# Norms and value parts that read the PSUM bank themselves, and buffers given back when their transfers should have landed

## The chip, the cores and the metric

The kernel runs on one core of a Trainium2 chip. A core has five engines that take instructions from queues of their own: TensorE (PE, matrix products into eight PSUM banks), VectorE (DVE), ScalarE (ACT), GpSimdE (POOL) and SyncE (SP), which here issues every DMA. The metric is the device time of one execution in microseconds (us). It was 2167.8 us, the median of three runs (2167.16 to 2171.36).

## The reference

One layer of a decoder runs over a prompt of 2048 positions and over 32 sample positions (8 sequences of 4 new tokens with caches). The input is RMS-normalised and projected by one wide matrix `w_in` to queries, keys, values, gates and mixing factors. Two attention branches read the projections:

- branch A: a causal window of 128, 8 query heads on 2 key/value heads, with a learned sink per head;
- branch B: three groups of 8 heads with (window, dilation) = (128, 1), (512, 4), (2048, 16), so that each query reads 128 keys, strided. The three outputs are weighted by their softmax denominators.

Queries and keys are normalised per head before use:

```python
def qk_norm(a, g, scale=1.0):
    a32 = a.astype(jnp.float32)
    y = a32 * lax.rsqrt(jnp.mean(a32 * a32, axis=-1, keepdims=True) + EPS)
    return (y * g.astype(jnp.float32) * scale).astype(a.dtype)
```

```python
s = jnp.einsum('nbqhgd,nbchd->nbhgqc', qb, kc, preferred_element_type=jnp.float32)
p, l, m = softmax_stats(s + bias, mask[None, :, None, None], sink)
o = jnp.einsum('nbhgqc,nbchd->nbqhgd', p, vc.astype(jnp.float32))
```

Both branches pass a SiLU gate and an up-projection, are merged by sigmoid factors, projected by `w_out` and added to the input. Besides the outputs, the last window rows of keys (after the norm and its gain) and values are returned for the caches: all 2048 rows of the group with dilation 16, 512 of the group with dilation 4, 128 of the others.

## The kernel before

**Split numbers.** Every float32 operand of a large product is written as the sum of two float16 parts, high and low, and a product is three float16 matmuls (high x high, high x low, low x high). `split` makes the parts: ACT writes the high part (L303), DVE subtracts it from the source for the low part (L306 or L308).

**Stages.** First the input is normalised and the mixing gates are computed (to about 390 us). Then come the three dilated groups, dilation 16, 4 and 1, with 16 tiles of 128 positions each; then branch A with the gates, also 16 tiles; then up- and output projections (from about 1800 us). In the dilation-16 group a tile attends only to itself (`nk` = 1), in the others mostly to two tiles of keys (`nk` = 2). In parallel with each group, the sample positions are attended from the caches, with products on POOL (L1172) and loads on SP.

**A tile.** `b_tile` gives a tile three projections: queries, keys, values. `proj` sums each in one PSUM bank with 24 matmuls of 512 columns (L259, the line of the helper `mm`). Five banks rotate among the projections and small transposes (`pbank`, `tbank`); in A, projections may hold only four of them (`most[0] = 4`). Scores use banks 3 and 4, values bank 7. When a bank is full, its chain starts:

- `q_chain` and `k_chain` call `norm`. ACT copies the bank into an SBUF buffer (L730) and the bank is given back; ACT squares that copy into scratch (L738); DVE sums per head (L740) and adds a constant (L741); POOL raises to the power -1/2 (L743) and, for queries, multiplies the gains in (L747); DVE multiplies the copy by the result (L751). The copy lies in `sq` for queries and `stK` for keys, the scratch and the later float16 parts in `qn` and `kn`.
- `parts` splits the result, and one DMA transpose (`SP.turn`, L167) turns it, queries into `QT`, keys into `KT`. `k_turn` then makes a second key layout with two DVE copies of half the partitions each (L773).
- If the tile's rows are returned, `k_rows` multiplies `stK` by the gain on POOL (L977) and stores it to DRAM.
- `v_chain` copies the bank to `stV` (L999), gives the bank back, waits for the tile before to have done its values, splits `stV` into one of two value buffers `VT`, and stores `stV` if the rows are returned.

`attend` then issues units of heads: scores (PE), bias and row maximum (DVE, L801), a scaling of the maxima (ACT, L810), exponentials (ACT, L815), split, a turn of the probabilities by DMA, and values (PE, 64-column matmuls). `finish` copies bank 7 and the softmax statistics into `Ut` (L1011, L1012), which is stored to DRAM.

**What sets the order.** The kernel is written as concurrent generators over a planned clock (`Clock`). The clock has a time at which each engine is free and an estimate of when a DMA lands (`ck.come`). A generator yields the planned time at which it wants to go on; whichever is due first emits its instructions next. The order of emission is the order in each engine's queue. Buffers and banks are guarded by planned locks (`sq_l`, `qn_l`, `kn_l`, `stK_l`, `Ut_l`, the banks' `lock`). The plan decides only the order: on the chip, an instruction waits by semaphores for whatever it really depends on, and all that is behind it in its engine's queue waits too. Before the change most locks of buffers under transfer are given back when the DMA is issued; `turn` waits until `ck.come`.

Of the kernel before, what the change touches and what calls it, by code (L numbers as in the profile page):

```python
# [13 lines left out]
F16 = mybir.dt.float16  # L14
# [6 lines left out]
P = 128  # L21
# [8 lines left out]
CW = 528  # L30
# [120 lines left out]
def hybrid_kernel(ctx, tc, xp, xs, ca, cb1, cb2, cb3, rel_bias, norm_gain, w_in, qga, kga, sinks, qgb, kgb,  # L151
# [541 lines left out]
    Ps = [cv(2, 512, dt=F16) for _ in range(2)]  # L693
    A_OP1 = cv.off
    Ut = cv(CW)
    stK, stV = cv(512), cv(512)
    A_OP0 = A_OP1 + 1024
    op = [arena[:, A_OP0:A_OP0 + 1024], arena[:, A_OP1:A_OP1 + 1024]]
    cv = Carve(A_OP0 + 1024)
    cb = cv(3, CW)  # L700
    SAMP = cv.off
    A_STV = A_OP1 + CW + 1024
    VTa = [x.rearrange("p a b -> p (a b)")[:, 640:].rearrange("p (a b) -> p a b", a=3) for x in VT]
    kv = kn[:, 128:384]

    sq_l, qn_l, kn_l, U_l, Ut_l, stK_l, stV_l, cb_l, fst_l = (Lock(ck) for _ in range(9))
    S_l, Sb_l, Ps_l, op_l = ([Lock(ck), Lock(ck)] for _ in range(4))
    PT_l = [Lock(ck) for _ in range(3)]
    unit_n = [0]
# [13 lines left out]
    start.scored = start.valued = start.finished = True  # L723
    start.biased = 4

    def norm(src, p0, n, nh, blk, scr, dst, gains=None, raw=None):


        if raw:
            A.activation(dst, src, AF.Copy)  # L730
            src = dst
            yield use("A", ta(nh * 64))
            raw[0].put()
            yield from raw[1].get()
        st = nst[p0:p0 + n, nrm_n[0] % 5]
        nrm_n[0] += 1
        s = scr[p0:p0 + n, :nh * 64]
        A.activation(s, src, AF.Square)  # L738
        yield use("A", ta(nh * 64))
        V.tensor_reduce(st[:, 0, :nh], heads(s), axis=AX.X, op=OP.add)  # L740
        V.tensor_scalar(st[:, 1, :nh], st[:, 0, :nh], 1.0 / 64, blk.epsc[p0:p0 + n], op0=OP.mult, op1=OP.add)  # L741
        yield use("V", tv(nh * 64) + 140)
        G.tensor_tensor(st[:, 2, :nh], st[:, 1, :nh], nhalf[p0:p0 + n].to_broadcast([n, nh]), op=OP.pow)  # L743
        f = use("G", 250 + 170 * nh)
        r = st[:, 2, :nh, None].to_broadcast([n, nh, 64])
        if gains is not None:
            G.tensor_tensor(heads(s), r, gains.to_broadcast([n, nh, 64]), op=OP.mult)  # L747
            f = use("G", tg(nh * 64))
            r = heads(s)
        yield f  # L750
        V.tensor_tensor(heads(dst), heads(src), r, op=OP.mult)  # L751
        yield use("V", tv(nh * 64))
# [16 lines left out]
    def k_turn(nh, dst, cur):  # L769
        x, y = (v[:, :, cur] for v in dst)  # L770
        yield from turn(x, kn, nh)
        for j in range(2):
            V.tensor_copy(y[64 - 64 * j:128 - 64 * j], x[64 * j:64 * j + 64])  # L773
            e = use("V", 33 * nh + 65)
        yield e

    def unit(t, y, n3, us, last):


        g, nk, cur = t.g, t.nk, t.cur  # L780
        w = nk * P
        nm, l, m = t.st[:, 0], t.st[:, 1], t.st[:, 2]
        xs_ = slice(2 * us[0], 2 * us[-1] + 2)
        hs = [(2 * u + j, u, j) for u in us for j in range(2)]
        sb = Sb[:, y]
        for a, (x, u, j) in enumerate(hs):
            for p_ in range(2):
                ks = t.KT[p_][:, x if g else j]
                ks = ks.rearrange("p s t -> p (s t)") if nk == 2 else ks[:, cur]
                mm(bank[3 + y][:, a * w:(a + 1) * w], t.QT[:, x], ks, p_ == 0, p_ == 1, cost(w))  # L790
        if last:
            t.scored = True
        yield ck.now + ck.LAT
        yield from Sb_l[y].get()
        for a, (x, u, j) in enumerate(hs):
            h = t.head(u, j)
            o, i_, b_ = sb[:, a * w:(a + 1) * w], bank[3 + y][:, a * w:(a + 1) * w], bias[:, h, (2 - nk) * P:]
            if nk == 2 and cur == 0:
                o, i_ = (v.rearrange("p (s t) -> p s t", s=2) for v in (o, i_))
                b_ = bass.AP(tensor=b_.tensor, offset=b_.offset + P, ap=[b_.ap[0], [-P, 2], [1, P]])  # L800
            V.tensor_tensor_reduce(out=o, in0=i_, in1=b_, scale=1.0,  # L801
                                   scalar=-3e38 if g else sinkS[:, u, j:j + 1], op0=OP.add, op1=OP.max,
                                   accum_out=m[:, x:x + 1])
            e = use("V", tv(w) + 80)
        t.used.update(us)
        while t.biased in t.used:
            t.biased += 1
        yield e
        S_l[y].put()
        A.activation(nm[:, xs_], m[:, xs_], AF.Copy, scale=ninv[:, g:g + 1])  # L810
        use("A", 200)
        t.nmd += len(us)
        for a, (x, u, j) in enumerate(hs):
            e = sb[:, a * w:(a + 1) * w]
            A.activation(e, e, AF.Exp, bias=nm[:, x:x + 1], scale=inv[:, g:g + 1], accum_out=l[:, x:x + 1])  # L815
            f = use("A", 0.833 * w + 372)
        yield f
        yield from Ps_l[y].get()
        yield from split(Ps[y][:, 0], Ps[y][:, 1], sb, 2.0 ** 14, 512)
        Sb_l[y].put()  # L820
        yield from PT_l[n3].get()
        pt = PT[n3]
        SP.turn(pt.rearrange("p b (a t) -> p (b a) t", t=P), Ps[y].rearrange("p b c -> p (b c)"))
        yield ck.come
        Ps_l[y].put()
        yield ck.now + 1800
        yield from cond(ck, lambda: t.v and t.prev.finished)
        for a, (x, u, j) in enumerate(hs):
            h = t.head(u, j)
            vc = (h if g else j) * 64  # L830
            o = bank[7][:, h * 64:h * 64 + 64]
            for n in range(nk):
                s = t.vslot(n if nk == 2 else cur)
                q = a * w + n * P
                ph, pl = (pt[:, z, q:q + P] for z in (0, 1))
                vh, vl = (t.VT[z][:, s, vc:vc + 64] for z in (0, 1))
                mm(o, ph, vh, n == 0, False, 27)
                mm(o, ph, vl, False, False, 27)
                mm(o, pl, vh, False, n == nk - 1, 27)
        PT_l[n3].put()  # L840
# [113 lines left out]
    def bcast_rows(row, n):  # L954
        return row[:, None, :].to_broadcast([n, 8, 64])

    def b_tile(g, t, tok, rows, nk, cur, last, par):
        t.g, t.nk, t.cur = g, nk, cur
        t.st = ast[:, par]
        t.QT, t.KT, t.VT = QT[(len(made) - 1) % 3], KT, VT  # L960
        t.head = lambda u, j: 2 * u + j
        t.vslot = lambda s: s
        prev = t.prev
        old = prev.prev and prev.prev.prev

        def q_chain(b):
            yield from sq_l.get()
            yield from norm(b.ap[:, :], 0, P, 8, blocks[f"q{g}"], qn, sq, GR[:, g % 2:g % 2 + 1], (b.lock, qn_l))
            yield from parts(qn, sq, 8, 1.0)
            sq_l.put()  # L970
            yield from cond(ck, lambda: old is None or old.scored)
            yield from turn(t.QT, qn, 8)
            qn_l.put()
            t.q = True

        def k_rows():
            G.tensor_tensor(heads(stK), heads(stK), bcast_rows(gk_row[:, g % 2], P), op=OP.mult)  # L977
            yield use("G", tg(512))
            SP.dma_start(rows[:, :512], stK)
            stK_l.put()  # L980
            t.kept = True

        def k_chain(b):
            yield from stK_l.get()
            yield from norm(b.ap[:, :], 0, P, 8, blocks[f"k{g}"], kn, stK, raw=(b.lock, kn_l))
            yield from parts(kn, stK, 8, 2.0 ** 11)
            if rows is None:
                stK_l.put()
# [5 lines left out]
            t.k = True  # L994

        def v_chain(b):
            yield from stV_l.get()
            blk = blocks[f"v{g}"]
            A.activation(stV, b.ap[:, :], AF.Copy, scale=2.0 ** -20 if rows is None else blk.c)  # L999
            yield use("A", ta(512, 1))  # L1000
            b.lock.put()
            yield from cond(ck, lambda: prev.valued)
            yield from split(VT[0][:, cur], VT[1][:, cur], stV, 1.0 if rows is None else blk.vs, 512)
            if rows is not None:
                SP.dma_start(rows[:, 512:], stV)
            stV_l.put()
            t.v = True

        def finish():
# [5 lines left out]
            def store():  # L1015
                yield e
                SP.dma_start(comb[g][tok], Ut)
                Ut_l.put()
                t.stored = True

            ck.spawn(store())
# [15 lines left out]
    sampB = samp_carve(A_STV, prod2=None)  # L1037
    cv = Carve(sampB["end"])
    KT.append(cv(8, 2, P, dt=F16))
    QT.append(cv(8, P, dt=F16))  # L1040
    sampA = samp_carve(SAMP, PT=A_PT, prod2=arena[:, A_SP:A_SP + 512],
                      Sr=arena[:, A_K + 1536:A_K + 1808])
# [311 lines left out]
    def a_tile(i, t, par):  # L1354
# [1 line left out]
        cur = i % 2  # L1356
        t.g, t.nk, t.cur = 0, 2 if i else 1, cur
        t.st = ast[:, par]
        t.QT, t.KT, t.VT = QT[1 - par], KTa, VTa
        t.head = lambda u, j: u + 4 * j  # L1360
        t.vslot = lambda s: (i if s == cur else i - 1) % 3
        t.ob = t.ga = t.gb = t.gs = t.cb = t.placed = False
        op_x = i % 2
        o = op[op_x]
# [22 lines left out]

        def q_chain(b):
            yield from sq_l.get()
            yield from norm(b.ap[:, :], 0, P, 8, blocks["q0"], qn, sq, GR[:, 0:1], (b.lock, qn_l))  # L1390
            yield from parts(qn, sq, 8, 1.0, True)
            sq_l.put()
            yield from cond(ck, lambda: prev.prev.scored)
# [453 lines left out]
```

## Time and profile before

| | before |
|---|---|
| median of three runs | 2167.8 us (2167.16 to 2171.36) |
| profiled execution: its time, its span | 2170.46 us, 2168.6 us |
| busy PE / DVE / ACT / POOL | 2029.2 / 1386.0 / 1053.3 / 707.9 us |
| mean granted TensorE clock | 0.979 |
| DMA | 344.34 MB, mean 159 GB/s |

A profile's span runs from the first to the last instruction. A row of a group names line, engine, operation, output and inputs, shapes and count; behind the bar stand total us and mean ns of one, behind the second bar the idle time of the engine just before, and what ended it. `arena` is the large SBUF buffer of which nearly all working buffers are parts, so `sq`, `stK`, `kn` and the rest all appear under that name; `bank` is a PSUM bank. In a timeline, a bracket gives the idle time before an instruction and what ended it. `SPq` is SP issuing a DMA.

### The profile page before, as it was taken

How to read it: one execution, taken by the hardware profiler on the slowest of the kernel's cores; microseconds unless marked ns; L12 is line 12 of the kernel's file. 1: busy time of each engine (PE TensorE's matmuls, PEld its weight loads, DVE VectorE, ACT ScalarE, POOL GpSimd, SP SyncE). 2: the span in 40 equal slices, each digit the busy share in tenths (PEclk: the TensorE clock that was granted, in tenths of full speed). 3: DMA queues.
4: the chain of work that ended last, by engine and by line, in shares of the span. 5: the costliest groups of instructions: out<-in, count | busy, mean ns of one | idle time of the engine just before them, and what ended most of it. 6: DMA issues, size and time to landing. Idle time of an engine off the chain costs nothing.

```text
span 2168.6 us, 36145 instructions
## 1 busy us (share of the span) xinstructions
PE 2029.2 (94%) x13042; PEld 1135.8 (52%) x13042; DVE 1386.0 (64%) x3305; ACT 1053.3 (49%) x2526; POOL 707.9 (33%) x530
## 2 busy tenths in 40 slices
PE   6999999999999899898999999997899997999999
PEld 3555555666665455554544554544455555444464
DVE  5546662576754577773767885869788898642331
ACT  5432312555555667665776766765456555300000
POOL 1000000255632245541324552426655653220110
PEclk9999999999999999999999999999999998999999
DMA  7896571368879568978857878744434366332322
GB/s 225 175 300 230 203 269 57 115 175 201 217 174 264 139 134 203 215 157 228 218 113 151 168 167 160 172 102 107 79 82 108 96 176 175 110 107 88 115 85 93
DMA packets 528389, 344.34 MB, mean 159 GB/s; under 512 B 397585, under 2 KB 427762, under 8 KB 528210
## 3 DMA queue, kind: packets, MB, share of 16 engines
q1 hardware_dynamic: 528210, 342.04, 61.4%
q8 instruction: 102, 1.67, 0.3%
q14 instruction: 77, 0.63, 0.1%
HBM read 193.53 MB, written 62.43 MB: 118 GB/s over the span
## 4 chain that ended last, share of the span: by engine, by line
PE 59%; DVE 15%; DMA 12%; ACT 5%; issue 4%; SPq 2%; POOL 2%; DVEq 0%; POOLq 0%; ACTq 0%
PE bank L259 58%; DMA arena<-arena 7%; DVE arena L308 3%; DVE arena L773 2%; DMA out_dram<-arena 2%; DVE slot L473 2%; DVE arena L801 2%; ACT arena L815 2%; SPq L161 1%; SPq L167 1%; ACT slot L470 1%; DMA hT<-arena 1%; ACT arena L303 1%; DVE arena L751 1%; POOL nst L743 1%
## 5 line engine op out<-in xcount | busy, mean ns | idle before, releaser
L259 PE MATMUL bank<-slot,hT 128*128 128x512 f16 (+1 forms) x4992 | 1127.6, 377 | 8.0 <-ACT arena L730 4.5
L259 PEld LDWEIGHTS <-hT 128*128 128x128 f16 x4992 | 546.8, 113 | 436.5 <-issue 45.2
L259 PE MATMUL bank<-hT,slot 128*128 128x416 f16 (+4 forms) x2928 | 530.8, 342 | 17.7 <-DVE slot L473 3.8
L743 POOL TENSOR_TENSOR nst<-nst,nhalf 128x8 f32<-128x8 f32 (+2 forms) x136 | 232.4, 1710 | 773.9 <-DVE nst L741 704.6
L259 PEld LDWEIGHTS <-slot 128*128 128x128 f16 x2928 | 287.2, 99 | 251.1 <-DVE slot L473 11.1
L259 PEld LDWEIGHTS <-arena 128*128 128x128 f16 x4336 | 267.9, 99 | 283.1 <-issue 88.9
L259 PE MATMUL bank<-arena 128*128 128x64 f16 (+5 forms) x3746 | 269.9, 230 | 88.6 <-DVE arena L773 44.5
L815 ACT ACTIVATE arena<-arena,ast,inv 128x256 f32<-128x256 f32 (+1 forms) x512 | 283.8, 555 | 7.0
L308 DVE SCALAR_TENSOR_TENSOR arena<-arena 128x512 f16<-128x512 f32 (+1 forms) x292 | 221.6, 772 | 92.2 <-ACT arena L303 91.2
L303 ACT ACTIVATE arena<-arena 128x512 f16<-128x512 f32 (+2 forms) x395 | 231.3, 607 | 98.6 <-DMA arena<-arena 53.8
L1172 POOL TENSOR_TENSOR arena<-arena 128x512 f32<-128x512 f32 (+1 forms) x102 | 140.1, 1373 | 120.7 <-DVE arena L1215 101.4
L259 PE MATMUL bank<-slot,arena 128*128 128x512 f16 x768 | 167.9, 379 | 2.1 <-DVE slot L473 1.6
L473 DVE SCALAR_TENSOR_TENSOR slot<-slot,gsc 128x512 f16<-128x512 f32 (+1 forms) x144 | 107.3, 745 | 86.7 <-ACT slot L470 86.2
L730 ACT ACTIVATE arena<-bank 128x512 f32<-128x512 f32 x112 | 65.8, 589 | 173.4 <-PE bank L259 89.4
L643 ACT ACTIVATE arena<-bank,wst 128x416 f32<-128x416 f32 (+2 forms) x82 | 48.7, 597 | 190.5 <-PE bank L259 162.9
L470 ACT ACTIVATE slot<-slot,gsc 128x512 f16<-128x512 f32 (+1 forms) x144 | 98.1, 681 | 73.2 <-DVE slot L473 63.7
L303 ACT ACTIVATE arena<-arena,yk 128x512 f16<-128x512 f32 (+2 forms) x40 | 25.5, 638 | 201.1 <-POOL arena L1706 186.4
L1706 POOL TENSOR_TENSOR arena<-arena 128x512 f32<-128x512 f32 (+2 forms) x40 | 48.7, 1218 | 221.2 <-DVE arena L1692 201.7
L801 DVE CUSTOM_DVE_ANT_0 arena<-bank,bias 128x128 f32<-128x128 f32 (+1 forms) x296 | 87.4, 343 | 50.2 <-PE bank L259 48.9
L740 DVE TENSOR_REDUCE nst<-arena 128x8 f32<-128x512 f32 (+2 forms) x136 | 85.6, 630 | 42.3 <-ACT arena L738 41.6
L773 DVE COPY arena<-arena 64x1024 f16<-64x1024 f16 (+1 forms) x128 | 77.5, 605 | 54.0 <-DMA arena<-arena 52.3
L810 ACT ACTIVATE ast<-ast,ninv 128x2 f32<-128x2 f32 (+1 forms) x212 | 61.2, 289 | 102.6 <-DVE ast L801 101.7
(167 smaller groups left out, 1758.5 us busy)
## 6 DMA issues: line engine op xcount, KB each, us to landing
arena<-in_cache_b_kv_dram SPq DMA_DIRECT2D x144, 256.0 KB
slot<-in_w_in_dram SPq DMA_DIRECT2D x64, 512.0 KB
arena<-Qs SPq DMA_DIRECT2D x96, 256.0 KB
arena<-in_w_in_dram SPq DMA_DIRECT2D x16, 1024.0 KB
gates<-arena SPq DMA_DIRECT2D x78, 208.0 KB
comb<-arena SPq DMA_DIRECT2D x48, 264.0 KB
arena<-comb SPq DMA_DIRECT2D x48, 264.0 KB
arena<-gates SPq DMA_DIRECT2D x24, 512.0 KB
```

Source lines behind the costliest of these rows:

```text
L259: T.matmul(out, l, r, start=start, stop=stop)
L303: A.activation(hi, src, AF.Copy, scale=scale)
L308: V.scalar_tensor_tensor(lo, src, scale, hi, op0=OP.mult, op1=OP.subtract)
L470: A.activation(b.part(0, k), src, AF.Copy, scale=sc)
L473: V.scalar_tensor_tensor(b.part(1, k), src, sc, b.part(0, k), op0=OP.mult, op1=OP.subtract)
L730: A.activation(dst, src, AF.Copy)
L740: V.tensor_reduce(st[:, 0, :nh], heads(s), axis=AX.X, op=OP.add)
L743: G.tensor_tensor(st[:, 2, :nh], st[:, 1, :nh], nhalf[p0:p0 + n].to_broadcast([n, nh]), op=OP.pow)
L773: V.tensor_copy(y[64 - 64 * j:128 - 64 * j], x[64 * j:64 * j + 64])
L801: V.tensor_tensor_reduce(out=o, in0=i_, in1=b_, scale=1.0, scalar=-3e38 if g else sinkS[:, u, j:j + 1], op0=OP.add, op1=OP.max, accum_out= ...
L815: A.activation(e, e, AF.Exp, bias=nm[:, x:x + 1], scale=inv[:, g:g + 1], accum_out=l[:, x:x + 1])
L1172: G.tensor_tensor(sprod[:n], q, k, op=OP.mult)
```

## The change

Four things differ.

1. `norm` no longer copies the bank. The square (ACT) and the last multiply (DVE) both read the bank, which is given back after that multiply. The chains take the scratch lock (`qn_l`, `kn_l`) before the norm. This holds for queries of all stages and keys of the three groups; keys of A and samples keep their way.
2. `v_chain` of the groups splits straight out of the bank, with a third value buffer `V3`, so that it waits for the values of the tile two before. `stV` is gone. If the rows are returned, a scaled copy goes from the bank into `Ut`, and is stored from there.
3. The locks of `stK` and `Ut` are given back 1200 ns after the planned landing of the store, and the lock of `Ps` (the probabilities' parts) 1200 ns after that of their turn. For `Ps` the following pause is shortened by as much, so the values keep their planned time.
4. `k_turn` waits 1200 ns more in the plan, behind the planned landing, before it emits the two copies.

```diff
-    def norm(src, p0, n, nh, blk, scr, dst, gains=None, raw=None):
-        if raw:
-            A.activation(dst, src, AF.Copy)
-            src = dst
-            yield use("A", ta(nh * 64))
-            raw[0].put()
-            yield from raw[1].get()
+    def norm(src, p0, n, nh, blk, scr, dst, gains=None):
...
     def k_turn(nh, dst, cur):
         x, y = (v[:, :, cur] for v in dst)
         yield from turn(x, kn, nh)
+        yield ck.now + 1200
...
-        yield ck.come
+        yield ck.come + 1200
         Ps_l[y].put()
-        yield ck.now + 1800
+        yield ck.now + 600
...
+    def v_at(z, s):
+        return V3[:, z] if s == 2 else VT[z][:, s]
...
+        t.vn = (len(made) - 1) % 3
-        t.vslot = lambda s: s
+        t.value = lambda z, s: v_at(z, t.vn if s == cur else t.prev.vn)
...
         def q_chain(b):
             yield from sq_l.get()
-            yield from norm(b.ap[:, :], 0, P, 8, blocks[f"q{g}"], qn, sq, GR[:, g % 2:g % 2 + 1], (b.lock, qn_l))
+            yield from qn_l.get()
+            yield from norm(b.ap[:, :], 0, P, 8, blocks[f"q{g}"], qn, sq, GR[:, g % 2:g % 2 + 1])
+            b.lock.put()
...
             SP.dma_start(rows[:, :512], stK)
+            yield ck.come + 1200
             stK_l.put()
...
         def k_chain(b):
             yield from stK_l.get()
-            yield from norm(b.ap[:, :], 0, P, 8, blocks[f"k{g}"], kn, stK, raw=(b.lock, kn_l))
+            yield from kn_l.get()
+            yield from norm(b.ap[:, :], 0, P, 8, blocks[f"k{g}"], kn, stK)
+            b.lock.put()
...
         def v_chain(b):
-            yield from stV_l.get()
-            blk = blocks[f"v{g}"]
-            A.activation(stV, b.ap[:, :], AF.Copy, scale=2.0 ** -20 if rows is None else blk.c)
-            yield use("A", ta(512, 1))
+            yield from cond(ck, lambda: prev.prev is None or prev.prev.valued)
+            yield from split(v_at(0, t.vn), v_at(1, t.vn), b.ap[:, :], 2.0 ** -20, 512)
+            if rows is not None:
+                yield from Ut_l.get()
+                A.activation(Ut[:, :512], b.ap[:, :], AF.Copy, scale=blocks[f"v{g}"].c)
+                yield use("A", ta(512, 1))
+                SP.dma_start(rows[:, 512:], Ut[:, :512])
+                ck.at(ck.come + 1200, Ut_l.put)
             b.lock.put()
-            yield from cond(ck, lambda: prev.valued)
-            yield from split(VT[0][:, cur], VT[1][:, cur], stV, 1.0 if rows is None else blk.vs, 512)
-            if rows is not None:
-                SP.dma_start(rows[:, 512:], stV)
-            stV_l.put()
             t.v = True
...
                 SP.dma_start(comb[g][tok], Ut)
-                Ut_l.put()
+                ck.at(ck.come + 1200, Ut_l.put)
...
     KT.append(cv(8, 2, P, dt=F16))
+    V3 = cv(2, 512, dt=F16)
```

The query chain of A (`a_tile`) is changed as that of `b_tile` is. The scratch of the samples moves down by the 512 words that `stV` had.

More of the change, by code (lines that the diff above doesn't have):

```diff
@@ L695, in hybrid_kernel @@
     Ut = cv(CW)
-    stK, stV = cv(512), cv(512)
+    stK = cv(512)
     A_OP0 = A_OP1 + 1024
@@ L701, in hybrid_kernel @@
     SAMP = cv.off
-    A_STV = A_OP1 + CW + 1024
+    A_STV = A_OP1 + CW + 512
     VTa = [x.rearrange("p a b -> p (a b)")[:, 640:].rearrange("p (a b) -> p a b", a=3) for x in VT]
     kv = kn[:, 128:384]
-    sq_l, qn_l, kn_l, U_l, Ut_l, stK_l, stV_l, cb_l, fst_l = (Lock(ck) for _ in range(9))
+    sq_l, qn_l, kn_l, U_l, Ut_l, stK_l, cb_l, fst_l = (Lock(ck) for _ in range(8))
     S_l, Sb_l, Ps_l, op_l = ([Lock(ck), Lock(ck)] for _ in range(4))
@@ L832, in unit @@
             for n in range(nk):
-                s = t.vslot(n if nk == 2 else cur)
+                s = n if nk == 2 else cur
                 q = a * w + n * P
                 ph, pl = (pt[:, z, q:q + P] for z in (0, 1))
-                vh, vl = (t.VT[z][:, s, vc:vc + 64] for z in (0, 1))
+                vh, vl = (t.value(z, s)[:, vc:vc + 64] for z in (0, 1))
                 mm(o, ph, vh, n == 0, False, 27)
@@ L959, in b_tile @@
         t.st = ast[:, par]
-        t.QT, t.KT, t.VT = QT[(len(made) - 1) % 3], KT, VT
+        t.QT, t.KT = QT[(len(made) - 1) % 3], KT
+        t.vn = (len(made) - 1) % 3
         t.head = lambda u, j: 2 * u + j
-        t.vslot = lambda s: s
+        t.value = lambda z, s: v_at(z, t.vn if s == cur else t.prev.vn)
         prev = t.prev
@@ L1358, in a_tile @@
         t.st = ast[:, par]
-        t.QT, t.KT, t.VT = QT[1 - par], KTa, VTa
+        t.QT, t.KT = QT[1 - par], KTa
         t.head = lambda u, j: u + 4 * j
-        t.vslot = lambda s: (i if s == cur else i - 1) % 3
+        t.value = lambda z, s: VTa[z][:, (i if s == cur else i - 1) % 3]
         t.ob = t.ga = t.gb = t.gs = t.cb = t.placed = False
@@ L1389, in q_chain @@
             yield from sq_l.get()
-            yield from norm(b.ap[:, :], 0, P, 8, blocks["q0"], qn, sq, GR[:, 0:1], (b.lock, qn_l))
+            yield from qn_l.get()
+            yield from norm(b.ap[:, :], 0, P, 8, blocks["q0"], qn, sq, GR[:, 0:1])
+            b.lock.put()
             yield from parts(qn, sq, 8, 1.0, True)
```

## The prediction

> **What bounds the kernel now.** I read the page's busy times first.
>
> ```profile
> PE 2029.2 (94%) x13042; PEld 1135.8 (52%) x13042; DVE 1386.0 (64%) x3305; ACT 1053.3 (49%) x2526; POOL 707.9 (33%) x530
> ```
>
> TensorE (PE) is busy 94% of the span, and no matmul is added or taken away. The change can only move the 139 us in which PE is not busy, and the granted clock. Next the busy times by stage: the three dilated groups (393 to 740, 740 to 1080, 1080 to 1420 us), branch A with the gates (1420 to 1830). Columns: window, length, busy us of PE, weight loads, DVE, ACT, POOL, then clock and DMA.
>
> ```profile
> 393.00:740.00 347.00, 322.37 (x1979) 204.89 (x1978) 216.51 (x556) 196.19 (x495) 155.00 (x103) 0.97 0.72 188
> 740.00:1080.00 340.00, 315.39 (x2177) 173.45 (x2177) 235.63 (x581) 222.69 (x554) 132.94 (x89) 0.97 0.80 190
> 1080.00:1420.00 340.00, 322.82 (x2351) 169.09 (x2349) 260.43 (x616) 242.42 (x600) 142.99 (x98) 0.99 0.75 157
> 1420.00:1830.00 410.00, 369.45 (x2745) 218.68 (x2745) 345.20 (x894) 225.79 (x612) 213.59 (x175) 0.95 0.48 115
> ```
>
> PE is idle for 66.4 us in the three groups (347.00 - 322.37, and so on) and 40.6 us in A; the diff touches nothing outside. No other engine is near its limit in the groups; in A, DVE works 84%. So the question is which waits stop PE. The waits of PE in the groups (first three rows), PE's in A, and ACT's in the groups; columns are total us, times, longest:
>
> ```profile
> PE bank L259 <- DVE arena L773: 33.1, 26, 4.7
> PE bank L259 <- DMA arena<-arena: 18.3, 17, 3.9
> PE bank L259 <- DVE ast L801: 6.0, 4, 3.1
> ...
> PE bank L259 <- DVE arena L773: 11.4, 6, 4.1
> ...
> ACT arena L730 <- DMA out_dram<-arena: 80.1, 13, 10.6
> ACT arena L999 <- DMA out_dram<-arena: 24.0, 7, 10.3
> ```
>
> Two things stand out. Score matmuls wait for the copies of the turned keys (L773), 44.5 us in 32 waits. And ACT, which takes its instructions in order, stands 104.1 us (80.1 + 24.0) at the copies out of a bank (L730, L999), because their destination is still being stored to DRAM.
>
> **Part 1: turned keys copied 1200 ns later in the plan.** `k_turn` gains a pause behind the turn. It adds no instruction; the planner emits the two copies, and behind them the tile's scores, after some 1.2 us more of other work. One ordinary tile:
>
> ```profile
> 548.04 3.18 SPq L167 DMA_TRANSPOSE arena<-arena  x2
> 552.37 2.24 DVE L773 COPY arena<-arena 64x1024 f16<-64x1024 f16 x2 [1.60 <-DMA arena<-arena]
> 554.67 0.55 PE L259 MATMUL bank<-arena 128*128 128x128 f16 x7 [0.94 <-DVE arena L773]
> ```
>
> The turn was issued at 548.04 and the copy could start at 552.37, DVE standing 1.60 us at it; PE then lost 0.94 us. With 1.2 us more projection ahead of the scores this wait is gone. The long L773 waits, and three others that have one cause with them:
>
> ```profile
> 689.47 0.91 PE L259 MATMUL bank<-arena 128*128 128x128 f16 x7 [4.72 <-DVE arena L773]
> 713.09 5.24 PE L259 MATMUL bank<-slot,hT 128*128 128x512 f16 x12 [4.53 <-ACT arena L730]
> 740.83 0.55 PE L259 MATMUL bank<-arena 128*128 128x128 f16 x7 [3.36 <-DVE arena L773]
> 811.75 0.49 PE L259 MATMUL bank<-arena 128*128 128x256 f16 x3 [1.95 <-DVE arena L773]
> 820.41 0.90 PE L259 MATMUL bank<-arena 128*128 128x256 f16 x4 [3.14 <-DVE ast L801]
> 911.09 0.91 PE L259 MATMUL bank<-arena 128*128 128x128 f16 x7 [3.79 <-DVE arena L773]
> 998.41 1.07 PE L259 MATMUL bank<-arena 128*32 128x512 f32 x8 [2.20 <-ACT arena L999]
> 1113.23 0.49 PE L259 MATMUL bank<-arena 128*128 128x256 f16 x3 [1.99 <-DVE arena L773]
> ...
> 1469.62 1.44 PE L259 MATMUL bank<-arena 128*128 128x256 f16 x15 [2.71 <-DVE arena L773]
> 1502.15 1.39 PE L259 MATMUL bank<-arena 128*128 128x256 f16 x11 [4.15 <-DVE arena L773]
> 1568.59 1.44 PE L259 MATMUL bank<-arena 128*128 128x256 f16 x15 [3.04 <-DVE arena L773]
> ```
>
> Eight of these are L773 waits and hold 25.7 us; the other 24 share 44.5 - 25.7 = 18.8 us, 0.78 us each. A delay of 1.2 us covers nearly all of these: 17.5 us. Of five long ones (811.75, 1113.23 and the three in A) it covers 1.2 us each: 6.0. Term 1 is 23.5 us; at most it is 18.8 + 3.9 + 9.9 = 32.6, and at worst a loss of 4.8, if only the last tile of each of four stages ends 1.2 us later. I take 23.5, near the upper end, since the delay equals the lateness the row shows. What is late next: values follow their scores at the same distance on PE as before, so turns of probabilities (18.3 us, second row of the waits) neither gain nor lose by it. SP's queue gets the probability turns 1.2 us later too, behind sample fetches it would otherwise precede.
>
> **Part 2: the stores.** The chain of waits around 689 (start, us, what):
>
> ```profile
> 678.15 5.28 DMA out_dram<-arena
> ...
> 683.51 0.60 ACT arena L730
> ...
> 688.25 1.18 DVE arena L773
> ...
> 689.47 0.58 PE bank L259 x4
> ```
>
> The K chain's raw copy into `stK` stood at the head of ACT until the last key store had landed; squares, weight conversions and exponentials queued behind it, and PE stopped for 4.72 us. I followed the other five of the same kind (713.09, 740.83, 820.41, 911.09, 998.41) back along that chain, and each has a store landing under ACT. Together 21.7 us. After the change nothing on ACT writes `stK`: the first write is the norm's last multiply on DVE, some 5 us down the chain, and the lock returns only when the plan thinks the store landed, plus 1.2 us. Values no longer pass `stV`; stored ones use `Ut`, held likewise. So ACT's 104 us go, and PE's 21.7 mostly; some of those waits had a second cause just behind, so I take three quarters, 16.3, between 0 and 21.7.
>
> **Part 3: clock.** Behind the 4.72 us gap and, for comparison, away from gaps (columns as above):
>
> ```profile
> 690.00:697.00 7.00, 7.00 (x34) 3.53 (x35) 4.69 (x22) 4.77 (x16) 2.01 (x1) 0.70 0.84 236
> 730.00:737.00 7.00, 7.00 (x44) 3.86 (x43) 2.00 (x2) 0.66 (x1) 1.64 (x1) 1.00 1.05 150
> ```
>
> At 0.70 PE lost 2.1 us of work that it counted as busy. Six such gaps are 12.6 us, and three quarters of that is 9.4; I take 8, since not every gap is as long. Bounds: 0, and the whole deficit of the four stages (0.03 x 347 + 0.03 x 340 + 0.01 x 340 + 0.05 x 410 = 44.5).
>
> **Part 4: norms and values read the bank.** By form (total us, mean ns after the bar):
>
> ```profile
> L730 ACT ACTIVATE arena<-bank 128x512 f32<-128x512 f32 x112 | 65.8, 589 | 173.4 <-PE bank L259 89.4 <-DMA out_dram<-arena 80.1 <-issue 3.7
> L751 DVE TENSOR_TENSOR arena<-arena 128x512 f32<-128x512 f32 x64 | 60.0, 937 | 6.7 <-POOL arena L747 6.5
> L751 DVE TENSOR_TENSOR arena<-arena,nst 128x512 f32<-128x512 f32 x48 | 43.5, 907 | 5.0 <-POOL nst L743 5.0
> L1459 DVE TENSOR_TENSOR arena<-arena,bank 128x512 f32<-128x512 f32 x16 | 10.9, 681 | 7.0 <-PE bank L259 7.0
> ```
>
> The 112 copies (65.8 us of ACT) go. Of the 48 value copies the 21 of stored tiles stay (now into `Ut`), 27 go. The multiplies now have one operand in a bank; the nearest row is L1459 at 681 ns, so DVE saves 64 x 0.256 + 48 x 0.226 = 27 us. In the groups all this is worth nothing by itself, since PE covers it (PE 93 to 95% busy, DVE at most 77%); without that cover it would be worth 27 us. In A only the 16 query multiplies change: 4.1 us of DVE, of which I give PE 2 (bounds 0 and 4.1).
>
> [...]
>
> What it costs is the bank. A query and a key norm before:
>
> ```profile
> 547.50 0.60 ACT L730 ACTIVATE arena<-bank 128x512 f32<-128x512 f32 x1 [1.08 <-PE bank L259]
> 555.26 0.60 ACT L730 ACTIVATE arena<-bank 128x512 f32<-128x512 f32 x1 [6.50 <-PE bank L259]
> 556.11 0.69 DVE L751 TENSOR_TENSOR arena<-arena 128x512 f32<-128x512 f32 x1
> 560.84 0.85 DVE L751 TENSOR_TENSOR arena<-arena,nst 128x512 f32<-128x512 f32 x1
> L259 PE MATMUL bank<-slot,hT 128*128 128x512 f16 (+1 forms) x4992 | 1127.6, 377 | 8.0 <-ACT arena L730 4.5 <-ACT slot L470 2.1 <-ACT arena L1409 0.7
> ```
>
> Banks came free 0.60 us after the first read; now only with the multiply: 556.80 - 547.50 = 9.3 us for the query, 561.69 - 555.26 = 6.4 for the key. PE is queued behind: the next projection into that bank, and everything after it in PE's order. A projection takes 24 x 1127.6 / 4992 = 5.4 us and five banks rotate, so a bank is wanted again after four others, 21.7 us. The cover is 12 us, and I cost the hold at nothing. If it is gone, one projection per tile waits for the excess: 1.5 us in each of 48 tiles would be 72 us. That is the upper bound.
>
> **Sum.** 23.5 + 16.3 + 8 + 2 = 49.8 us saved. PE reaches the probability turns and L801 with less slack; I let those waits (24.3 us in the groups) grow by a quarter, 6.1. Net 43.7. The profiled execution took 2170.5 us (its span 2168.6 and 1.9 around it), 2.7 above the median of 2167.8. So 2126.8 for an execution like it, 2124 for the median.
>
> **Rivals.**
> 1. *All of it arrives*: 32.6 + 21.7 + half the clock deficit, 22 = 76 us: about 2092. For it: PE has work at hand wherever it waited. Against: it needs turns of 4 us always to land inside the plan.
> 2. *The waits only move*: the gain returns as longer waits for probability turns and softmax, 18.3 + 6.0 us in the groups now; they would have to triple: about 2166. For it: the SP queue stays one queue. Against: those chains start at the scores, which keep their distance.
> 3. *Slower, by held banks*: multiplies stuck on DVE behind the key copies, or key chains holding a bank while waiting for `stK`, keep a bank over 21.7 us. From there 72 us less the 43.7: about 2196. For it: in the 9.3 us above DVE spent 1.60 us standing at L773 and 2.24 on it, and A leaves projections only four banks with DVE at 84%. Against: the cover of 12 us. [...]
>
> **Chances.** Forecast with its own range 2105 to 2155: 0.60. Rival 1: 0.17. Rival 2: 0.09. Rival 3: 0.14. The range 2090 to 2172 leaves out the far end of rival 1 and most of rival 3. Faster by over 0.2% (4.3 us, about what a measurement of this kernel can tell from no change): 0.77; within: 0.09; slower: 0.14.
>
> **What would show it.** Right: PE's waits for L773 fall from 44.5 to under 15 us; ACT's waits for stores fall from 104 to under 15; the group windows show PE idle under 45 us and clocks of 0.98 or more; no PE wait for the norm's multiply (L751) over 5 us in total. Wrong: PE waits for the norm's multiply or for the square at a new projection (rival 3), or longer PE waits for turns and L801 (rival 2). If L773 waits stay, the planner's delay does not reach PE's order.

## The result and the profile after

The changed kernel takes 2111.35 us (median; 2110.55 to 2116.05), against 2167.48 us (2164.9 to 2171.36) for the kernel before on the same chip: a ratio of 0.9744, 95% interval 0.9724 to 0.9765, or 56 us less. The forecast was 2124 us in a range of 2090 to 2172.

The page of the changed kernel, busy times, then how its span divides:

```profile
span 2110.0 us, 35983 instructions
...
PE 2006.8 (95%) x13042; PEld 1129.3 (54%) x13042; DVE 1367.9 (65%) x3305; ACT 981.4 (47%) x2387; POOL 704.6 (33%) x530
```

The same 13042 matmuls take 22.4 us less of busy time (2029.2 to 2006.8), and PE's idle time falls by 36.2 us (2168.6 - 2029.2 = 139.4 to 103.2). Together that is the whole 58.6 us between the two spans. Most of the busy part is the clock, whose mean rose from 0.979 to 0.988: by the trace's records of it, TensorE was at half clock for 92.2 us of the span before and for 51.2 us after, and half of that difference is 20.5 us. The windows of before, now on the changed kernel:

```profile
393.00:740.00 347.00, 335.39 (x2100) 214.22 (x2099) 223.93 (x594) 189.88 (x497) 159.09 (x108) 1.00 0.82 195
740.00:1080.00 340.00, 331.45 (x2403) 181.41 (x2402) 242.12 (x619) 215.88 (x548) 135.83 (x93) 1.00 0.86 198
1080.00:1420.00 340.00, 324.31 (x2395) 174.73 (x2393) 262.49 (x647) 217.09 (x554) 157.99 (x111) 0.98 0.73 154
```

Over these 1027 us PE is idle for 35.9 us instead of 66.4. (The third window now holds the first tiles of A, which starts earlier.) PE's waits in the changed kernel, longest in total first, then those at 393 to 1420 us that the norm's last multiply (L744 here) ends:

```profile
PE bank L259 <- DMA arena<-arena: 26.9, 21, 5.3
PE bank L259 <- DVE arena L767: 15.3, 12, 5.0
```

```profile
PE bank L259 <- DVE arena L744: 2.3, 3, 1.3
```

The waits for the key copies (L773 before, L767 here) fell from 44.5 us to 15.3. Those for turned probabilities stayed as they were (27.8 before), and a projection rarely waits for a norm to give a bank back. By form, the new multiplies and the copies that are left:

```profile
L744 DVE TENSOR_TENSOR arena<-bank,arena 128x512 f32<-128x512 f32 x64 | 43.8, 685 | 22.8 <-POOL arena L740 22.7
L744 DVE TENSOR_TENSOR arena<-bank,nst 128x512 f32<-128x512 f32 x48 | 32.9, 686 | 8.9 <-POOL nst L736 8.7
L731 ACT ACTIVATE arena<-bank 128x512 f32<-128x512 f32 x112 | 65.8, 590 | 110.2 <-PE bank L259 77.8 <-DMA arena<-arena 32.2
```

The multiply takes 685 ns (937 and 907 before), the squares 590 ns, and the 112 copies are gone. ACT no longer waits for a store to `out_dram` at all. It waits elsewhere instead: 32.2 us at the squares, whose scratch an earlier turn still reads (3.8 us before), and 4.3 us at the copies into `Ut`, for that buffer's store to `comb`.

The end of the three groups is read from the last of the 48 copies of bank 7 (L1011 before, L1013 after). Behind the durations a row gives the first and the last start:

```profile
L1011 ACT ACTIVATE arena<-bank,wst x48: 662/668/691, 439.8 to 1431.8; 128x512 f32<-128x512 f32 x48
```

```profile
L1013 ACT ACTIVATE arena<-bank,wst x48: 663/682/699, 436.9 to 1370.8; 128x512 f32<-128x512 f32 x48
```

Counted from 393 us, just behind the gates in both, the groups took 1038.8 us and now take 977.8: all of the gain, 61 us. From there, branch A up to its last product with bank 7 (L1459, L1464) takes 423 us now and took 417 before; it gained nothing.

### The profile page after: what moved, and what is told of

Read it like the earlier page. It is cut to its first block, busy times and chain, and to the rows that moved or that the text cites. A ratio compares the mean times of both kernels' runs of the same rounds, so it can differ in the third digit from the quotient of the medians.

```text
span 2110.0 us, 35983 instructions
## 1 busy us (share of the span) xinstructions
PE 2006.8 (95%) x13042; PEld 1129.3 (54%) x13042; DVE 1367.9 (65%) x3305; ACT 981.4 (47%) x2387; POOL 704.6 (33%) x530
## 4 chain that ended last, share of the span: by engine, by line
PE 67%; DVE 14%; DMA 8%; ACT 4%; issue 3%; POOL 2%; SPq 2%; DVEq 0%; POOLq 0%; ACTq 0%
PE bank L259 65%; DMA arena<-arena 5%; DVE arena L308 3%; DVE arena L795 2%; DVE slot L473 1%; ACT arena L809 1%; DMA hT<-arena 1%; SPq L161 1%; SPq L167 1%; ACT arena L303 1%; DMA arena<-comb 1%; DVE arena L767 1%; ACT slot L470 1%; POOL nst L736 1%; PE bank L885 1%
## 5 line engine op out<-in xcount | busy, mean ns | idle before, releaser
L259 PE MATMUL bank<-slot,hT 128*128 128x512 f16 (+1 forms) x4992 | 1114.7, 373 | 7.9 <-DVE arena L1435 4.8
L736 POOL TENSOR_TENSOR nst<-nst,nhalf 128x8 f32<-128x8 f32 (+2 forms) x136 | 221.2, 1627 | 715.0 <-DVE nst L734 329.1
L259 PEld LDWEIGHTS <-arena 128*128 128x128 f16 x4336 | 263.3, 98 | 234.2 <-DMA arena<-arena 37.3
L259 PE MATMUL bank<-arena 128*128 128x64 f16 (+5 forms) x3746 | 262.7, 227 | 44.5 <-DMA arena<-arena 26.9
L303 ACT ACTIVATE arena<-arena 128x512 f16<-128x512 f32 (+2 forms) x368 | 218.1, 607 | 127.1 <-DVE arena L744 89.6
L308 DVE SCALAR_TENSOR_TENSOR arena<-arena 128x512 f16<-128x512 f32 (+1 forms) x292 | 227.6, 792 | 67.7 <-ACT arena L303 66.8
L731 ACT ACTIVATE arena<-bank 128x512 f32<-128x512 f32 (+2 forms) x120 | 70.2, 587 | 115.2 <-PE bank L259 77.8
L795 DVE CUSTOM_DVE_ANT_0 arena<-bank,bias 128x128 f32<-128x128 f32 (+1 forms) x296 | 87.4, 343 | 41.8 <-PE bank L259 41.2
L1755 DVE SCALAR_TENSOR_TENSOR slot<-bank,sst,slot 128x512 f32<-128x512 f32 (+1 forms) x33 | 24.8, 751 | 125.6 <-PE bank L259 115.9
```

What stands on the lines that cost most here:

```text
L259: T.matmul(out, l, r, start=start, stop=stop)
L303: A.activation(hi, src, AF.Copy, scale=scale)
L308: V.scalar_tensor_tensor(lo, src, scale, hi, op0=OP.mult, op1=OP.subtract)
L795: V.tensor_tensor_reduce(out=o, in0=i_, in1=b_, scale=1.0, scalar=-3e38 if g else sinkS[:, u, j:j + 1], op0=OP.add, op1=OP.max, accum_out= ...
```

## The experiments

My theory had three parts: the pause ahead of the key copies saves PE's short waits (23.5 us), ACT no longer standing at stores saves the long ones (16.3 us), and the norms reading the bank are worth next to nothing in the groups (2 us in A). Its rivals gave other parts the gain. The first four kernels do one part alone on the kernel before. Each ratio is against the kernel before, timed along with it.

**The pause alone.**

```diff
         yield from turn(x, kn, nh)
+        yield ck.now + 1200
```

> The kernel before with one edit: the key copies (L773) are planned 1200 ns later. My theory, term 1: PE's waits for L773 fall from 44.5 us to under 20, ACT's waits for stores stay near 104 us, and the time falls by 15 to 28 us, to about 2145. Rival, the gain of the whole change comes from ACT no longer standing at stores: L773 waits only move to the turns of probabilities, and the time falls by less than 6 us.

Measured: 2201.62 us, ratio 1.0114 (1.0087 to 1.0141). Slower, which neither theory had. PE's waits, and ACT's for stores in the groups:

```profile
PE bank L259 <- DVE arena L774: 38.9, 19, 7.1
PE bank L259 <- DMA arena<-arena: 37.5, 21, 5.6
PE bank L259 <- ACT arena L1000: 12.3, 4, 7.1
...
PE bank L259 <- ACT arena L730: 8.7, 5, 6.0
```

```profile
ACT arena L730 <- DMA out_dram<-arena: 91.5, 16, 9.6
...
ACT arena L1000 <- DMA out_dram<-arena: 52.9, 14, 9.6
```

The key copies stop PE 19 times instead of 32, but for longer each, and the waits for banks that ACT has not yet copied (L1000, L730) grow from 6.7 to 21.0 us, while ACT stands 144 us at stores instead of 104. The pause did take short waits away; in this order of work others came.

**The norms alone.**

```diff
-            A.activation(dst, src, AF.Copy)
-            src = dst
-            yield use("A", ta(nh * 64))
-            raw[0].put()
-            yield from raw[1].get()
...
+            yield from kn_l.get()
+            yield from norm(b.ap[:, :], 0, P, 8, blocks[f"k{g}"], kn, stK)
+            b.lock.put()
```

> The kernel before with one edit: query and key norms read the bank, which is given back after the norm's multiply; locks are given back at the issue of a store as before. My theory: since the first write to the key buffer is now the multiply on DVE, ACT's waits for stores at the norm fall from 80 us to under 10 without any lock being held longer, and PE's waits behind them go; minus 10 to 18 us, about 2154. Rival, the lock given back at issue is what matters: the wait goes over to the multiply (DVE stands over 30 us for stores), and the time falls by less than 6 us. Rival of held banks: PE waits for the multiply, slower than before.

Measured: 2128.22 us, ratio 0.9777 (0.9752 to 0.9803). One part gives 47 us, more than twice the upper end of what I had expected. PE's waits, then ACT's for stores:

```profile
PE bank L259 <- DVE arena L767: 19.8, 24, 1.6
PE bank L259 <- DMA arena<-arena: 19.2, 17, 3.0
...
PE bank L259 <- DVE ast L795: 5.4, 3, 3.8
```

```profile
ACT arena L997 <- DMA out_dram<-arena: 51.8, 12, 7.6
```

Without any pause the waits for key copies fell to 19.8 us, none longer than 1.6. The 80 us that ACT stood at the key store are gone as expected, but at the value copies ACT now stands 51.8 us (24.0 before), and the kernel is fast all the same.

**The late locks alone** (the diff leaves out `Ut` and `Ps`, which are treated alike).

```diff
             SP.dma_start(rows[:, :512], stK)
+            yield ck.come + 1200
             stK_l.put()
...
-            stV_l.put()
+                ck.at(ck.come + 1200, stV_l.put)
```

> The kernel before with one edit: the key, value and output buffers under store, and the probabilities' parts under their turn, are given back 1200 ns after the planned landing. My theory: banks are held by the plan instead of ACT standing; ACT's waits for stores fall from 104 us to under 35 and the time falls by 8 to 16 us, about 2156. Rival, the stores land later than the plan thinks by more than 1200 ns: ACT's waits for stores stay over 60 us and the time within 5 us of before.

Measured: 2169.01 us, ratio 0.9973 (0.9958 to 0.9987). ACT's waits for stores at a norm or value copy, and PE's waits:

```profile
ACT arena L730 <- DMA out_dram<-arena: 6.8, 5, 2.8
```

```profile
PE bank L259 <- DMA arena<-arena: 37.2, 33, 4.6
PE bank L259 <- DVE arena L773: 23.5, 28, 2.3
```

ACT's 104 us fell to 6.8, the waits for key copies to 23.5 us, and the time only by 0.27%: PE waits longer for turned probabilities instead (27.8 to 37.2 us), and its whole idle time in the profiled execution is 143.9 us, not less than the 139.4 before. This is the run that takes my second step apart. ACT standing at a store stopped PE in single places, as the chain of waits showed, but taking the standing away did not give those microseconds back.

**The values alone** (straight from the bank, third buffer, stored from `Ut`, locks given back at issue).

> The kernel before with one edit: values are split straight from the bank into one of three buffers, stored ones also copied to the output buffer and stored from there, locks given back at issue. My theory: this alone is worth little, since value chains were not on PE's waits but for one of 2.2 us: minus 0 to 8 us, about 2164; with the output buffer given back at issue ACT may stand at it instead (up to 24 us of ACT waits for stores). Rival: the third value buffer is what frees the plan, and over 15 us go.

Measured: 2168.59 us, ratio 0.9983 (0.9961 to 1.0005): no difference, as expected. ACT stands 14.2 us at the copies into `Ut`. The next four kernels take one part out of the change, or put the copy back.

**The change without the pause.**

```diff
         yield from turn(x, kn, nh)
-        yield ck.now + 1200
```

> The changed kernel without the pause of 1200 ns ahead of the key copies. Theory: the pause helps only where ACT no longer stands at stores (alone it made the kernel 1.1% slower, with ACT's waits for stores up from 104 to 144 us). Then this is slower than the changed kernel by 8 to 20 us, ratio 0.978 to 0.984, with PE's waits for the key copies back at 20 to 30 us from 15.3. Rival, the pause is worth nothing in any surroundings: ratio 0.970 to 0.976.

Measured: 2131.16 us, 0.9807 (0.9781 to 0.9833). Inside the first theory's band; PE's waits for the key copies are back at 28.4 us. What this is worth is taken up at the last control.

**The change with locks given back at issue.**

```diff
             SP.dma_start(rows[:, :512], stK)
-            yield ck.come + 1200
             stK_l.put()
...
```

> The changed kernel with the locks of key, output and probability buffers given back at the issue of the transfer. Theory from the run with late locks alone (ACT's waits for stores from 104 to about 7 us, time 0.27% down): late locks are worth little by themselves; ratio 0.974 to 0.980, with ACT's waits for the stores of values (into the output buffer) back at 15 to 50 us. Rival, they carry the difference between the norm alone (0.978) and the whole change (0.974) and more, since DVE's multiply would stand at the key store: over 0.985.

Measured: 2132.97 us, 0.9822 (0.9794 to 0.9849), between the two bands. ACT waits 39.7 us at the copies into `Ut`, as the theory had it; the rival, which rested on DVE's multiply standing at the key store, needed a ratio over 0.985.

**The change with the copy kept in the norms** (the first diff lines of the norms put back, all else as after).

> The changed kernel with the norms copying the bank first, as before; pause, late locks and values from the bank stay. Theory: the norm carries nearly all of the gain, so this is near the kernel before, ratio 0.990 to 1.005, though ACT hardly waits for stores (under 20 us). Rival, the four parts add up in any order (-0.2, -0.3, +1.1, -2.2%): ratio 1.006 or more. Second rival, what matters is that ACT does not stand at stores: ratio under 0.982.

Measured: 2149.97 us, 0.9904 (0.9875 to 0.9933). At the lower edge of the band of the theory that the norm carries most of the gain. The four single ratios multiplied would give 0.984, and without the norm 1.007: the parts do not add up.

**The norms alone, with a copy that nobody reads.**

```diff
         s = scr[p0:p0 + n, :nh * 64]
+        if blk.name[0] == "q" and n == P or blk.name in ("k1", "k2", "k3") and n == P:
+            A.activation(s, src, AF.Copy)
+            yield use("A", ta(nh * 64))
         A.activation(s, src, AF.Square)
```

> The kernel with only the norm changed (0.978), plus a copy by ACT of each query and key bank into the scratch, which nobody reads (the square overwrites it); square and multiply still read the bank. It puts back the 66 us of ACT and the 0.6 us in each chain, and leaves the multiply from the bank, the free key buffer and the plan of the banks. Theory, ACT's time in the chain is what the norm saves: 20 to 35 us come back, ratio 0.987 to 0.995. Rival, it is the multiply from the bank (0.68 instead of 0.92 us on DVE) and ACT not standing at stores: ratio 0.975 to 0.982.

Measured: 2194.68 us, 1.0093 (1.0058 to 1.0127). The copy alone, 589 ns in each of 112 chains, gives the whole gain back and more, though the multiply still reads the bank and the key buffer is still free. That is beyond both bands, on the first theory's side. PE's waits:

```profile
PE bank L259 <- DMA arena<-arena: 46.9, 25, 15.5
PE bank L259 <- DVE arena L770: 27.9, 26, 4.5
```

The loss does not sit where the gain of the norms alone was. Against that kernel the waits at the key copies (L770 here) rise by only 8.1 us, those for turned probabilities by 27.7, and PE's busy time by 16.8 us at a lower clock (0.970 instead of 0.986).

**The norms alone, with the same work on ACT aside** (57 us in all, behind the chain's own ACT work, in the groups alone).

```diff
             yield from parts(kn, stK, 8, 2.0 ** 11)
+            if g:
+                for _ in range(2):
+                    A.activation(arena[:, 14776:14896], ident[:, :120], AF.Copy)
+                use("A", 590)
...
```

> The kernel with only the norm changed, plus the same work on ACT as a copy of a bank (two copies of 120 columns from a constant into unused words, about 0.6 us) for each query and key of the three groups, but behind the chain's own work on ACT, so that no chain waits for its result; only the time of the groups is compared (393 us to the last output copy: 1001 us with the norm alone, 1040 with the copy kept in the chain). Theory, the chain's length is what PE feels: groups 998 to 1012 us, ratio 0.975 to 0.985. Rival, ACT's load is: groups over 1030 us, ratio over 0.990.

Measured: 2151.15 us, 0.9898 (0.9869 to 0.9927), groups 1020.1 us. Between the bands of chain length (998 to 1012) and load (over 1030): it does not decide. Nor is the load quite the same: ACT's busy time in the groups rises by 41.8 us, against 50.8 with the copy in the chain.

The traces show what the copy does to the chain itself. I pair the n-th first read of a query or key bank with the n-th multiply of that kind, 96 pairs in the groups. From the start of the read to the end of the multiply the mean is 9.6 us before, 6.9 with the norms alone, 8.8 with the copy that nobody reads, 7.0 with the work aside and 7.2 in the change. So 0.59 us of copy lengthens a chain by nearly 2 us, and in the work-aside kernel the chains stay short while the groups take 18.7 us more than with the norms alone. If that is more than a difference of order, chain length is not all.

**A control: the pause at 1300 ns instead of 1200.**

> The changed kernel with the pause ahead of the key copies at 1300 ns instead of 1200: no step of any theory turns on 100 ns, so what it moves is what a mere reordering by the planner is worth here. Theory: within 6 us of the changed kernel, ratio 0.971 to 0.978. Rival, the plan's order is so touchy that single edits cannot be told from chance: more than 12 us off, ratio under 0.969 or over 0.980.

Measured: 2153.7 us, 0.9905 (0.9872 to 0.9937). A hundred nanoseconds in the plan cost 1.6%. No step of any theory turns on them; the instructions are the same, and the planner merely orders them differently, on ACT from about 418 us on, in the first group. PE's waits in this kernel:

```profile
PE bank L259 <- DMA arena<-arena: 36.7, 16, 7.3
PE bank L259 <- DVE arena L767: 16.2, 14, 3.1
PE bank L263 <- DVE arena L1343: 12.9, 2, 7.5
...
PE bank L259 <- DVE arena L744: 10.2, 4, 4.7
```

The key copies cost what they cost after the change (15.3 us). Others grew: turned probabilities, the transposes of A behind their scaling (L1343, 4.7 before the extra 100 ns), and 10.2 us at banks that a norm still held, up to 4.7 us at a time.

**The pause at 2400 ns.**

> The changed kernel with the pause at 2400 ns. Theory: with 1200 ns PE's waits for the key copies are already down to 12 (15.3 us), so a longer pause takes away at most some of these and ends each stage later; within 8 us of the changed kernel, ratio 0.971 to 0.979, waits for the copies under 12 us. Rival, the longer the better: under 0.968.

Measured: 2149.84 us, 0.989 (0.9858 to 0.9921); waits for the key copies 19.2 us. Outside both bands: not better, and worse by as much as the control.

**The values 1200 ns later.**

```diff
         Ps_l[y].put()
-        yield ck.now + 600
+        yield ck.now + 1800
```

> The changed kernel with the values planned 1200 ns later behind the turn of the probabilities (1800 instead of 600 ns after the lock is given back). Theory: PE's longest remaining waits in the tiles are those for the turned probabilities (26.9 us in 21 times); they fall by the same rule as the key copies did, to under 15 us, and 5 to 12 us go: ratio 0.968 to 0.973. Rival, later values hold the tiles up through the order of outputs (a tile starts only when the one two before has ended): 0.974 or more.

Measured: 2106.15 us, 0.9691 (0.9659 to 0.9723), the lowest time of all, and below the changed kernel's interval by a hair. The waits for turned probabilities fell from 26.9 us to 16.3, near the 15 of the theory, and the ratio lies in its band. With a control that moves 1.6%, this one order is no proof that later values are better as a rule.

**All orders together.** A single comparison of two orders is worth little here, but each kernel is one more draw. The time of the three groups, from 393 us to the last copy of bank 7:

| ACT copies the bank in the norm's chain | us | it does not | us |
|---|---|---|---|
| kernel before | 1038.8 | norms alone | 1001.4 |
| pause alone | 1070.8 | change without pause | 1000.7 |
| late locks alone | 1027.2 | change, locks at issue | 995.1 |
| values alone | 1031.5 | the change | 977.8 |
| change with copied norms | 1011.0 | pause 1300 | 1006.2 |
| norms alone, copy that nobody reads | 1039.8 | pause 2400 | 1018.7 |
| | | values later | 964.3 |
| mean | 1036.5 | mean | 994.9 |

The means differ by 41.6 us, with standard deviations of 20 and 18 within the columns, so a standard error of about 11 (the square root of 391/6 + 333/7); it is a rough one, since these are different edits and not orders drawn at random. The kernel with the work aside is in neither column; counted on the right, it makes the difference 38.5. Three pairs differ in the norms or their copy alone: before and norms alone (37.4 us), copied norms and the change (33.2), the copy that nobody reads and norms alone (38.4). The kernel before and the one with that copy differ by 1.0 us, so in these two orders reading the bank gains nothing while the copy stays in the chain. The copy out of the chain is worth some 33 to 42 us in the groups, beyond the 28.4 us by which the control moved them. What the other edits are worth singly cannot be read from these orders.

## Why the prediction was right and wrong

- **The total and its split between waits and clock.** Right in direction and near in size: 43.7 us forecast, 56 measured. Waits were to give 35.7 of it (49.8 less 8 for the clock and 6.1 returned), and PE's idle time fell by 36.2. That agreement is luck: alone, the two parts that were to give most of it cost 1.1% (the pause) or gave 0.27% (the late locks), and the part put at 2 us gave 2.2%. The clock term was mis-sized: 8 forecast, about 20 measured, with 1.00 granted in the first two groups where it had been 0.97. I had counted only six gaps at 2.1 us. Between 393 and 1830 us the clock records show 18 half-clock stretches before, 82 us in all, and 5 after, 37.5 us.
- **Part 4 is the step that failed.** "In the groups all this is worth nothing by itself, since PE covers it." The rows of part 4 were right: multiplies at 685 ns for the 681 taken, 27 us of DVE saved at the multiplies (60.0 + 43.5 to 43.8 + 32.9), 66 us of ACT gone. But they stand in the chain from a full bank to the key copies, and PE did not cover that chain: it waited at its end 32 times. I had priced the norms by how busy the engines are, when PE's largest wait named their chain's end. The norms alone gave 47 us and took 24.7 us off that wait, and the groups differ by 33 to 42 us between kernels with the copy and without. Putting 589 ns of copy back in the chain undid it, though mostly at other waits and by the clock. Whether ACT's load or the chain's length does it stays open: the run with the work aside fell between, and one order cannot settle it.
- **Part 1, the pause, 23.5 us.** The wait it aimed at did fall, to 15.3 us, but without it to 19.8 with the norms alone and to 28.4 in the change. Alone it made the kernel slower, and in the change its removal cost 0.6% (0.9744 to 0.9807), less than 100 ns more of it did (1.6%). Its worth is not separable from reordering. What failed in this step is the assumption behind it, that a delay moves one thing and leaves the rest in place.
- **Part 2, the stores, 16.3 us.** ACT's waits for stores went as forecast, but the late locks took them away alone (104 us to 6.8) and the time fell by 0.27%. A wait that stands on the chain that ended last was not a saving of that length: turned probabilities came late next (27.8 us to 37.2).
- **Rival 1**, all of it arrives (2092): no, though the clock part of it came. **Rival 2**, the waits only move: what late locks alone did, not the change. **Rival 3**, held banks: 2.3 us at the norms' multiply in the groups of the changed kernel, so the cover held: from its first read to the end of the multiply a bank is now kept 7.2 us in the mean and 12.3 at most, against the 21.7 of four projections. With the pause at 1300 ns such waits cost 10.2 us, 4.7 at once. The mechanism exists, at a seventh of the price. Copying each bank out at once is the slower choice here, by the ratio of 0.978 of the norms alone.
- **The signs named in advance**: idle PE in the group windows 35.9 us (under 45 forecast), ACT's waits for stores 5.9 us (all to `comb`), L744 2.3 us in the groups; L767 at 15.3, just over the 15 I had set; clock 0.98 or more.

## What to carry to other kernels

When the bounding engine's largest wait names the end of a chain, do not put an instruction of that chain at nothing because its engine is half idle: here 0.59 us of copy on ACT, 49% busy, made a chain nearly 2 us longer in the mean. In a kernel whose order of work comes out of a planner, time a meaningless change of the plan first: here 100 ns moved 1.6%, and only what held in three pairs and in the mean of thirteen kernels could be called an effect. Taking one wait away gained little where the next one stood behind it (0.27% by the late locks alone); look at the sum of the waits and the clock after the edit, and not only at the wait that the edit was for.

## What was not expected of the hardware

**Two SBUF operands beside POOL.** A multiply of two SBUF operands on DVE does not always take 0.69 us. Minimum, median and maximum in ns, of L751 before and of L744 after:

```profile
L751 DVE TENSOR_TENSOR arena<-arena x64: 671/687/1757, 400.3 to 1784.3; 128x512 f32<-128x512 f32 x64
```

```profile
L744 DVE TENSOR_TENSOR arena<-bank,arena x64: 672/684/693, 399.8 to 1722.6; 128x512 f32<-128x512 f32 x64
```

The medians are within 3 ns of each other (687 and 684), so by them a bank source costs nothing here; with one operand in a bank none of 64 took over 693 ns, and the whole saving of the mean (937 to 685) is the tail. One of the long ones stands beside the POOL instruction that began before it:

```profile
852.89 1.27 POOL L1172 TENSOR_TENSOR arena<-arena 128x512 f32<-128x512 f32 x1
852.97 1.74 DVE L751 TENSOR_TENSOR arena<-arena 128x512 f32<-128x512 f32 x1 [1.20 <-POOL arena L747]
```

In the groups before the change, 27 of 98 such multiplies with full tiles took over 1 us. Each of them began while POOL was at an instruction on 512 columns in SBUF (mostly L1172), and ended 0.55 us after it did. Five more, at 844 to 855 ns, show the same. Of the other 66, 51 lay beside no POOL instruction; six began ahead of such a POOL instruction, and nine lay beside POOL's power on 8 columns (L743), and all 66 took 674 to 693 ns. After the change 54 of 100 lay beside POOL, and none took over 693 ns.

**Where the clock was halved.** Between 393 and 1830 us the traces record 18 half-clock stretches before and 5 after, each 3.41 us long or two or three times that, 81.9 and 37.5 us in all. In the 3.41 us just ahead of each, PE had stood idle for 1.99 us or more in sum; the least was 1.99 us before (ahead of the stretch at 1421.31 us) and 2.01 us after (ahead of that at 1373.37 us). By an estimate from these lengths, 3.41 us at half clock are worth 1.7 us of PE's work, on top of the idling. That the idling is the cause is inferred from these 23 stretches; no run varied it alone.
